# A Hymba-style block on one core: the filters' second stage a step later, the gates' scaling on VectorE, and a reordered pass change and filters' start

## The chip, the cores and the metric

The kernel runs on one core of a Trainium2 chip. The core has TensorE (PE, matrix products), VectorE (DVE), ScalarE (ACT), GpSimd (POOL) and SyncE (SP, which here only issues transfers), each with an instruction stream of its own that is worked through in order. The metric is the time of one execution in microseconds on the device; lower is better. The median of several runs is taken.

## The reference, cut to what matters

One encoder block, with 2048 positions, 1024 channels, float32. Half of the projected channels go through a Fourier mix, the other half through a Hyena operator of order 2, whose long filters are generated by a small network and normalised.

```
def implicit_filters(l, w0, b0, w_inner, b_inner, freq, w_out):
    z, t = positional_features(l)
    h = jnp.sin(fr * (z @ w0 + b0))
    for j in range(FILTER_INNER_LAYERS):
        h = jnp.sin(fr * (h @ w_inner[j] + b_inner[j]))
    h = (h @ w_out).reshape(l, HYENA_ORDER, N_DIRECTIONS, HYENA_WIDTH)
    h = h * decay[:, None, None, :]
    k = jnp.concatenate([h_fwd[:1] + h_bwd[:1], h_fwd[1:], jnp.zeros_like(h_fwd[:1]),
                         h_bwd[1:][::-1]], axis=0)
    return k * lax.rsqrt(jnp.sum(k * k, axis=0, keepdims=True) + EPS)

def hyena_mix(u, ...):
    u = short_conv(u, conv_w, conv_b)
    x1, x2, v = jnp.split(u, HYENA_ORDER + 1, axis=-1)
    k_freq = jnp.fft.rfft(implicit_filters(...), axis=0)
    z = v
    for n, gate in enumerate((x1, x2)):
        z = gate * fft_long_conv(z, k_freq[:, n], long_d[n])
    return z

def reference(x, ...):
    p = rmsnorm(x, g_mix) @ w_in
    u_f, u_h = p[..., :512], p[..., 512:]
    y_f = rmsnorm(fourier_mix(u_f), g_fourier)
    y_h = rmsnorm(hyena_mix(u_h, ...), g_hyena)
    x = x + jnp.concatenate([y_f, y_h], -1) @ w_out
    x = x + jnp.square(jax.nn.relu(rmsnorm(x, g_mlp) @ w_fc1)) @ w_fc2
    return rmsnorm(x, g_final)
```

## The kernel before, in words

**Stages.** In order of time: pass 1 of the input projection (x1 and x2, with the filter network between its groups), pass 2 (the Fourier part and v, with loads of tables and sums of weights between its groups), the filters with the Fourier mix in their first steps, Hyena, the output projection and the two layers of the MLP. The 2048 positions are 16 tiles of 128. The scheduler of the program fixes the order of each engine's instructions when the kernel is built, by the order of the code, by priorities and by what depends on what; `behind` adds a fixed "this after that".

**The projection (`project`, L337 to L458).** Each float32 operand is split into a high and a low half (`xh`, `xl`; `wh`, `wl`), and `mm3` (L208 to L212) makes three products of them. A group is one position tile times one half of the columns: 8 x 3 = 24 products into `pu`. `parts` gives the order of the groups, `front` loads and splits a tile's activations (L197 makes `xl`), and `weights_in` splits the weights. Where the weights carry a gain (`gmix`), the low half is made on VectorE by L200, else by L197. `convolve` runs the short convolution: `term` (L378) on VectorE, additions on GpSimd (L401, L405, L414) and, in `finish` (L397), on VectorE; the results go to the tensor `gates` in DRAM (0 is v, 1 and 2 are x1 and x2). In pass 2 the groups of the Fourier part are copied into `uf`.

**The filters (`filters`, L526 to L689).** There are eight units: four tiles of 128 channels times two orders n. A unit has four steps of each kind. `generate` (L566) multiplies the network's last layer into `pk`, VectorE multiplies by the decay (L568), ScalarE squares (L580), and GpSimd sums the squares into `acc` (L582 to L585). `stage1` (L625) is the first stage of the filter's Fourier transform, and VectorE transposes its result into `Gk` (L629). `stage2` (L634) multiplies `Gk` by the table `f2`; ScalarE copies the result to `ks` (L637, three buffers), and SyncE writes 1 MB of it to `spec` in DRAM (L641). `generate` and `stage1` take turns with two PSUM buffers each (`pair`). `normalise` (L590 to L600) sums `acc` over the partitions with a product, and works out the scale factors `sc`, `dk` and `both` on VectorE; `skip` (L607 to L613) puts the skip weight in and broadcasts the norms of a channel tile into `norms`.

**The order in the filters.** A loop of 43 steps runs all of it: step s has generate s of the 32, stage 1 of seven steps before, and stage 2 of eleven steps before, so a unit's first stage 2 stands in the step behind its last stage 1. `ordered` ties every product to the one before, so TensorE follows the code. In steps 0 to 10, `FOURIER` says how many steps of the Fourier mix come first: L482 multiplies `uf` into `pf`, and L464 transposes that into `Gf`. In steps 24 to 27 (`LOAD`) the four column tiles of v are fetched from `gates` into `zz`, 1 MB each, on SyncE's queue, and in `SCALE`'s steps GpSimd multiplies a tile by `norms` in four pieces (L688). The decay tiles of unit 0 are loaded over ScalarE's queue, at a raised priority.

**Hyena (`hyena`).** It reads `zz`, `gates` and, over SyncE's queue, the spectra (`ks<-spec`, L719); L733 is its first product, L748 and L756 follow.

## Time and profile before

| what | value |
|---|---|
| runs | 2293.11, 2289.97, 2285.28 us; median 2289.97 us |
| the profiled execution | 2289.12 us, span 2287.3 us |
| mean granted clock of TensorE | 0.989 |
| pass change | about 226 to 250 us into the span |
| filters, with the Fourier mix | about 406 to 612 us |
| DMA | 477.00 MB, mean 209 GB/s |

The time of an execution is a little more than its span, because the span begins with the first and ends with the last recorded instruction. In a timeline row the columns are start, duration, engine, line, operation, result and operands, tile shape and count; in brackets stands how long the engine was idle before and what ended that. In a row of windows come the stretch, busy time and instructions of each engine, the granted clock, the busy share of the DMA engines and GB/s. In a row of groups, the columns are busy time in all and mean ns of one, then the idle time ahead of them with what ended it.

### The profile page before, as it was taken

The numbers are of one execution on the slowest core, as the hardware profiler recorded it, in microseconds if no ns is written. First come the engines' busy times: TensorE is split into PE (matmuls) and PEld (weight loads), VectorE is DVE, ScalarE is ACT, GpSimd is POOL, SyncE is SP. The second block draws the span as 40 slices with busy tenths as digits, with TensorE's granted clock in tenths as the row PEclk, the third lists the DMA queues.
The fourth block names the chain that finished last, engine by engine and source line by source line (L and its number), as shares of the span: only waits on it lengthen the run. The fifth ranks groups of instructions, "written<-read, shape, count | busy, mean of one in ns | idle before, by whom it ended". The sixth has DMA issues, their size and how long they took to land.

```text
span 2287.3 us, 34559 instructions
## 1 busy us (share of the span) xinstructions
PE 2203.4 (96%) x12881; PEld 1801.2 (79%) x12881; DVE 1458.6 (64%) x2172; ACT 1076.4 (47%) x1788; POOL 788.1 (34%) x607
## 2 busy tenths in 40 slices
PE   8999999987899989998999999999999999999998
PEld 6888788665688858887888878888888888888886
DVE  6999767654478774457444465444476666866667
ACT  6545111453366564456555565555533333533334
POOL 3434333456276611136655556555300000000000
PEclk9999999998999999999999999999999999999999
DMA  8535986568886766567444475444499766866631
GB/s 271 179 130 182 355 284 238 178 245 269 333 257 206 218 190 180 177 210 238 158 152 152 152 242 173 152 152 152 143 335 339 237 195 192 304 193 195 192 119 74
DMA packets 296505, 477.00 MB, mean 209 GB/s; under 512 B 17349, under 2 KB 141455, under 8 KB 292113
## 3 DMA queue, kind: packets, MB, share of 16 engines
q1 hardware_dynamic: 290097, 458.29, 60.4%
q10 hardware_dynamic: 6240, 16.51, 2.1%
q8 instruction: 101, 1.65, 0.3%
q14 instruction: 67, 0.55, 0.1%
HBM read 305.17 MB, written 168.00 MB: 207 GB/s over the span
## 4 chain that ended last, share of the span: by engine, by line
PE 70%; POOL 2%; DVE 2%; DMA 2%; ACT 2%; issue 2%; SPq 0%; POOLq 0%; ACTq 0%; DVEq 0%
PE p2u L210 5%; PE p2u L212 5%; PE p2u L211 5%; PE p1u L210 5%; PE p1u L212 5%; PE p1u L211 5%; PE p2v L210 3%; PE p2v L212 3%; PE p2v L211 3%; PE pz L733 2%; PE p1v L211 2%; PE p1v L210 2%; PE p1v L212 2%; PE po L210 2%; PE po L212 2%; PE po L211 2%
## 5 line engine op out<-in xcount | busy, mean ns | idle before, releaser
L196 ACT CAST qahm<-ra 128x1024 fp32r<-128x1024 f32 x110 | 115.9, 1053 | 344.0 <-PE p2u L211 172.0
L197 DVE TENSOR_TENSOR qalm<-ra,qahm 128x1024 fp32r<-128x1024 f32 x110 | 134.7, 1224 | 154.0 <-ACT qahm L196 152.4
L1297 POOL TENSOR_TENSOR acc<-acc,gfin 128x512 f32<-128x512 f32 x4 | 5.1, 1277 | 631.6 <-DMA out<-acc 624.4
L211 PE MATMUL pu<-wl,xh 128*128 128x512 f32 x512 | 201.6, 394 | 4.2 <-DVE wl L200 4.0
L210 PE MATMUL pu<-wh,xh 128*128 128x512 f32 x512 | 204.1, 399 | 0.7 <-ACT wh L199 0.7
L212 PE MATMUL pu<-wh,xl 128*128 128x512 f32 x512 | 201.6, 394 | 1.9 <-DVE xl L197 1.9
L211 PE MATMUL p2u<-qblm,qahm 128*128 128x512 f32 x504 | 196.1, 389 | 0.0
L210 PE MATMUL p2u<-qbhm,qahm 128*128 128x512 f32 x504 | 195.8, 389 | 0.0
L212 PE MATMUL p2u<-qbhm,qalm 128*128 128x512 f32 x504 | 195.7, 389 | 0.0
L197 DVE TENSOR_TENSOR qblm<-rb,qbhm 128x1024 fp32r<-128x1024 f32 x110 | 134.0, 1218 | 3.8 <-ACT qbhm L196 3.5
L401 POOL TENSOR_TENSOR acc<-acc,cw 128x512 f32<-128x512 f32 x45 | 59.5, 1321 | 200.7 <-DVE acc L378 197.4
L196 ACT CAST ahm<-s 128x512 fp32r<-128x512 f32 x124 | 76.7, 621 | 98.5 <-PE p1v L211 54.0
L197 POOL TENSOR_TENSOR alm<-W,ahm 128x512 fp32r<-128x512 f32 x63 | 87.7, 1393 | 94.1 <-ACT ahm L196 94.1
L196 ACT CAST qbhm<-rb 128x1024 fp32r<-128x1024 f32 x110 | 115.3, 1048 | 5.9 <-DMA rb<-in_w_fc 3.1
L211 PEld LDWEIGHTS pu<-wl,xh 128*128 128x128 f32 x512 | 97.2, 190 | 26.1 <-DVE wl L200 5.5
L212 PEld LDWEIGHTS pu<-wh,xl 128*128 128x128 f32 x512 | 97.1, 190 | 23.3 <-DVE xl L197 3.4
L210 PEld LDWEIGHTS pu<-wh,xh 128*128 128x128 f32 x512 | 97.3, 190 | 21.5 <-ACT wh L199 1.1
L210 PEld LDWEIGHTS p2u<-qbhm,qahm 128*128 128x128 f32 x504 | 94.6, 188 | 20.0 <-issue 0.3
L212 PEld LDWEIGHTS p2u<-qbhm,qalm 128*128 128x128 f32 x504 | 94.6, 188 | 19.7
L211 PEld LDWEIGHTS p2u<-qblm,qahm 128*128 128x128 f32 x504 | 94.6, 188 | 19.6
L210 PE MATMUL p1u<-bm,ahm 128*128 128x512 f32 x252 | 99.8, 396 | 7.6 <-ACT ku L1159 7.6
L196 ACT CAST ahm<-W 128x512 fp32r<-128x512 f32 x94 | 57.8, 617 | 97.9 <-PE p1u L211 95.4
(375 smaller groups left out, 6159.8 us busy)
## 6 DMA issues: line engine op xcount, KB each, us to landing
W<-in_w_fc SPq DMA_DIRECT2D x66, 512.0 KB, 4.7
spec<-ks SPq DMA_DIRECT2D x32, 1024.0 KB, 5.4
ks<-spec SPq DMA_DIRECT2D x64, 512.0 KB, 4.6
rb<-td SPq DMA_DIRECT2D x64, 512.0 KB, 10.1
ra<-a1m SPq DMA_DIRECT2D x56, 512.0 KB, 3.7
ra<-a0m SPq DMA_DIRECT2D x54, 512.0 KB, 3.8
rb<-in_w_fc SPq DMA_DIRECT2D x46, 512.0 KB, 10.7
f<-in_w_fc SPq DMA_DIRECT2D x16, 1024.0 KB, 6.0
```

Of the source, the lines that this page charges most:

```text
L196: nc.scalar.copy(hi, src)
L197: (eng or nc.vector).tensor_sub(lo, src, hi)
L210: nc.tensor.matmul(o, lhsT=lh, rhs=rh, start=start, stop=False, skip_group_check=more)
L211: nc.tensor.matmul(o, lhsT=lh, rhs=rl, start=False, stop=False, skip_group_check=more)
L212: nc.tensor.matmul(o, lhsT=ll, rhs=rh, start=False, stop=stop, skip_group_check=more)
L401: nc.gpsimd.tensor_add(m1, m1, cw[:, 3, :])
L733: nc.tensor.matmul(p[:, 256 * sp : 256 * sp + 256], lhsT=e1[:, sp, :], rhs=zz[:, :, lo : lo + 16], start=True, stop=True)
L1297: nc.gpsimd.tensor_mul(acc[i][:, c], acc[i][:, c], gfin[:, c])
```

## The change

In the filters, stage 2 comes twelve steps behind generate instead of eleven, and the loop has 44 steps. The scaling of `zz` by `norms` goes from GpSimd to VectorE, one piece of a tile in each step from 28 on. The reciprocal and the factors `dk` and `both` move from `normalise` into a new `scales`, which stands behind the products of its step; the square root stays in `normalise`. A small fill of one row goes from GpSimd to VectorE.

At the filters' start, unit 0's first generate is split into `raw` (products) and `multiply`: its products come before the first four Fourier products, and its multiplication behind the fourth transposition. The last two groups of pass 2 are exchanged, so that the Fourier part's group is last, and unit 0's decay loads stand behind that group's copy into `uf`. At the pass change, the first four groups of pass 2 are tied to run one after the other, and the second tile's `front` has a raised priority.

```
@@ project
         else:
             parts[:4] = (0, 0), (1, 0), (0, 1), (1, 1)
+            parts[-2:] = (15, 1), (15, 0)
...
-            for k in range(8):
-                mm3(p, xh[:, k, :], xl[:, k, :], *w[h, k], k == 0, k == 7)
+            group = [mm3(p, xh[:, k, :], xl[:, k, :], *w[h, k], k == 0, k == 7) for k in range(8)]
+            if uf is not None and 0 < at < 4:
+                behind([group[0][0]], end)
+            end = group[-1][1]
             for j in after[at]:
-                fronts[j] = front(order[j])
+                with ExitStack() if uf is None or at else tc.high_priority(offset=200):
+                    fronts[j] = front(order[j])
...
-                nc.scalar.mul(uf[:, t, :], p, r)
+                filled = nc.scalar.mul(uf[:, t, :], p, r)
...
+        if uf is not None:
+            line.append(filled)
@@ ordered
-        if line:
-            behind([x], line[-1])
-        line[:] = [x]
+        if len(line) > 1:
+            behind([x], line.pop())
+        line.append(x)
@@ Unit.decay
-                (nc.scalar if self.i == 0 else nc.sync).dma_start(decs[k], A["decay"][self.ct][:, 8 * k : 8 * k + 8, :])
+                d = (nc.scalar if self.i == 0 else nc.sync).dma_start(decs[k], A["decay"][self.ct][:, 8 * k : 8 * k + 8, :])
+                if self.i == 0:
+                    behind([d], line[0])
             def generate(self, k):
+                self.multiply(k, self.raw(k))
@@ Unit.multiply
-                nc.vector.tensor_mul(new, p.rearrange(...), decs[k].rearrange(...))
+                made = nc.vector.tensor_mul(new, p.rearrange(...), decs[k].rearrange(...))
+                if first is not None:
+                    behind([made], first)
...
-                    nc.gpsimd.memset(end, 0.0)
+                    nc.vector.memset(end, 0.0)
@@ Unit.normalise
-                self.sc = rsqrt(v, fp, "k", 8)
+                self.root = fp.tile([P, 1], F32, tag="sq_k", name="sq_k", bufs=2)
+                nc.scalar.sqrt(self.root, self.v)
+
+            def scales(self):
+                v = self.v
+                self.sc = rsqrt(v, fp, "k", 8, self.root)
@@ the steps
-        SCALE = {28: 0, 30: 1, 32: 2, 38: 3}
-        for step in range(43):
+        for step in range(44):
...
+            if step == 0:
+                begun = units[0].raw(0)
             if step < SOLO:
                 for _ in range(FOURIER[step]):
-                    next(fourier_steps)
-            u, q = divmod(step - 11, 4)
+                    out = next(fourier_steps)
+            if step == 0:
+                units[0].multiply(0, begun, out)
+            u, q = divmod(step - 12, 4)
...
-            if u < 8:
+            if 0 < step < 32:
                 units[u].generate(k)
...
+            u, q = divmod(step - 5, 4)
+            if 0 <= u < 8 and q == 0:
+                units[u].scales()
...
-            if step in SCALE:
-                j = SCALE[step]
-                for q in range(4):
-                    z = zzs[0][:, 4 * q : 4 * q + 4, 128 * j : 128 * j + 128]
-                    nc.gpsimd.tensor_mul(z, z, norms[:, j : j + 1, :].broadcast_to([P, 4, 128]))
+            j, q = divmod(step - 28, 4)
+            if j >= 0:
+                z = zzs[0][:, 4 * q : 4 * q + 4, 128 * j : 128 * j + 128]
+                nc.vector.tensor_mul(z, z, norms[:, j : j + 1, :].broadcast_to([P, 4, 128]))
```

Where the instructions come to stand is decided when the program is built. First VectorE at the pass change, in the order of before: the numbers tell buffers apart, `wl_2313` and `wl_2319` are low halves of the last two Fourier weights, `wl_2323` that of the first v weight.

```order
L397 TENSOR_TENSOR acc<-acc,m_2215 128x512
L197 TENSOR_TENSOR wl_2313<-st_2314,wh_2312 128x512
L197 TENSOR_TENSOR wl_2319<-st_2314,wh_2318 128x512
L378 SCALAR_TENSOR_TENSOR acc<-pu_2219,nw_s,cw_270 128x512
L378 SCALAR_TENSOR_TENSOR m_2248<-pu_2219,nw_s,cw_270 128x512
L378 SCALAR_TENSOR_TENSOR m_2250<-pu_2219,nw_s,cw_270 128x512
L397 TENSOR_TENSOR acc<-acc,early 128x512
L397 TENSOR_TENSOR acc<-acc,m_2250 128x512
L397 TENSOR_TENSOR last<-last,nb 128x512
L200 SCALAR_TENSOR_TENSOR wl_2323<-st,gmix,wh_2322 128x512
```

The same stretch of VectorE in the changed kernel (its lines L382 and L401 are L378 and L397 of before):

```order
L401 TENSOR_TENSOR acc<-acc,m_2215 128x512
L197 TENSOR_TENSOR wl_2303<-st_2304,wh_2302 128x512
L197 TENSOR_TENSOR wl_2309<-st_2304,wh_2308 128x512
L197 TENSOR_TENSOR wl_2313<-st_2314,wh_2312 128x512
L382 SCALAR_TENSOR_TENSOR acc<-pu_2219,nw_s,cw_270 128x512
L197 TENSOR_TENSOR xl<-xc,xh 128x1024
L382 SCALAR_TENSOR_TENSOR m_2248<-pu_2219,nw_s,cw_270 128x512
L382 SCALAR_TENSOR_TENSOR m_2250<-pu_2219,nw_s,cw_270 128x512
L401 TENSOR_TENSOR acc<-acc,early 128x512
L401 TENSOR_TENSOR acc<-acc,m_2250 128x512
L401 TENSOR_TENSOR last<-last,nb 128x512
L197 TENSOR_TENSOR wl_2319<-st_2314,wh_2318 128x512
```

The split of an activation tile (`xl`) has moved ahead, and the last Fourier weight's low half (`wl_2319`) stands behind the three additions of `finish`.

Second, TensorE around the first stage 2 of unit 0, before (L566 generate, L625 stage 1, L634 stage 2):

```order
L612 MATMUL pdiag<-diag,ones 128x128
L566 MATMUL pk<-wo,emb 32x128 x32
L625 MATMUL pk_4386<-k,e1k 32x512 x8
L634 MATMUL pk_4401<-Gk,f_2585 128x128 x4
L634 MATMUL pk_4408<-Gk,f_2585 128x128 x4
```

And in the changed kernel (there L578, L648 and L657):

```order
L635 MATMUL pdiag<-diag,ones 128x128
L578 MATMUL pk<-wo,emb 32x128 x32
L648 MATMUL pk_4386<-k,e1k 32x512 x8
L578 MATMUL pk<-wo,emb 32x128 x32
L648 MATMUL pk_4444<-k,e1k 32x512 x8
L657 MATMUL pk_4455<-Gk,f_2585 128x128 x4
L657 MATMUL pk_4462<-Gk,f_2585 128x128 x4
```

One generate and one stage 1 now stand between a unit's last stage 1 and its first stage 2.

Third, VectorE in steps 22 to 24 before, the products with the decay and the transpositions:

```order
L629 STREAM_TRANSPOSE Gk<-pk_5262 128x8x2x32 x2
L568 TENSOR_TENSOR k<-pk,dec_4737 128x8x8x16
L629 STREAM_TRANSPOSE Gk<-pk_5333 128x8x2x32 x2
L568 TENSOR_TENSOR k<-pk,dec 128x8x8x16
L576 TENSOR_TENSOR k<-k,lag_5394 1x8x16
L629 STREAM_TRANSPOSE Gk<-pk_5402 128x8x2x32 x2
```

And in the changed kernel, where L715 is the scaling (`dec_4723`, `pk_5319` and so on are the same buffers under new numbers):

```order
L652 STREAM_TRANSPOSE Gk<-pk_5248 128x8x2x32 x2
L583 TENSOR_TENSOR k<-pk,dec_4723 128x8x8x16
L715 TENSOR_TENSOR zz<-zz,norms 128x4x128 x2
L652 STREAM_TRANSPOSE Gk<-pk_5319 128x8x2x32 x2
L715 TENSOR_TENSOR zz<-zz,norms 128x4x128 x2
L583 TENSOR_TENSOR k<-pk,dec 128x8x8x16
L593 TENSOR_TENSOR k<-k,lag_5380 1x8x16
L594 MEMSET k 1x8x16
L652 STREAM_TRANSPOSE Gk<-pk_5388 128x8x2x32 x2
```

The first tile's four scalings, which on GpSimd stood behind sums of squares, stand two and two around the transpositions of step 23; the second and third tiles' eight follow in the same way over steps 25 and 26, and the fourth tile's four stand near the end of the filters.

More of the change, by code (lines that the diff above doesn't have):

```diff
@@ L208, in mm3, with rsqrt @@
     def mm3(o, lh, ll, rh, rl, start, stop, more=False):
-        nc.tensor.matmul(o, lhsT=lh, rhs=rh, start=start, stop=False, skip_group_check=more)
+        a = nc.tensor.matmul(o, lhsT=lh, rhs=rh, start=start, stop=False, skip_group_check=more)
         nc.tensor.matmul(o, lhsT=lh, rhs=rl, start=False, stop=False, skip_group_check=more)
-        nc.tensor.matmul(o, lhsT=ll, rhs=rh, start=False, stop=stop, skip_group_check=more)
-    def rsqrt(v, pl, nm, keep=None):
-        s, r = (pl.tile(list(v.shape), F32, tag=f"{a}_{nm}", name=f"{a}_{nm}") for a in ("sq", "rc"))
+        return a, nc.tensor.matmul(o, lhsT=ll, rhs=rh, start=False, stop=stop, skip_group_check=more)
+    def rsqrt(v, pl, nm, keep=None, s=None):
+        r = pl.tile(list(v.shape), F32, tag=f"rc_{nm}", name=f"rc_{nm}")
         q = pl.tile(list(v.shape), F32, tag=f"nw_{nm}{keep or ''}", name=f"nw_{nm}", bufs=keep)
-        nc.scalar.sqrt(s, v)
+        if s is None:
+            s = pl.tile(list(v.shape), F32, tag=f"sq_{nm}", name=f"sq_{nm}")
+            nc.scalar.sqrt(s, v)
         nc.vector.reciprocal(r, s)
@@ L335, in weights_in @@
         return w
+    line = []
     def project(ip, fx, cps, sets, uf):
@@ L482, in fourier @@
             ordered(nc.tensor.matmul(p, lhsT=e1f, rhs=ufv[:, :, :, 16 * c : 16 * c + 16], start=True, stop=True))
-            turned(G, c, p.rearrange("p (x c e) -> p c e x", c=8, e=2))
-            yield
+            yield turned(G, c, p.rearrange("p (x c e) -> p c e x", c=8, e=2))
         def rows(i):
@@ L566, in generate, with multiply @@
                                 ordered(nc.tensor.matmul(o, lhsT=w, rhs=wo[rows[h], self.n, cols], start=True, stop=True))
+                return p
+            def multiply(self, k, p, first=None):
                 new = self.k.rearrange("p c l j -> p l c j")[:, 8 * k : 8 * k + 8]
-                nc.vector.tensor_mul(new, p.rearrange("p q (l c j) -> p (q l) c j", l=4, c=8), decs[k].rearrange("p l (c j) -> p l c j", c=8))
+                made = nc.vector.tensor_mul(new, p.rearrange("p q (l c j) -> p (q l) c j", l=4, c=8), decs[k].rearrange("p l (c j) -> p l c j", c=8))
+                if first is not None:
+                    behind([made], first)
                 if self.n == 1 and self.i < 7:
```

6 lines of the change are left out of this document (3 added, 3 removed).

## The prediction

> **What bounds the kernel now.** I read the page's first part first: which engine has no time to spare.
>
> ```profile
> PE 2203.4 (96%) x12881; PEld 1801.2 (79%) x12881; DVE 1458.6 (64%) x2172; ACT 1076.4 (47%) x1788; POOL 788.1 (34%) x607
> ```
>
> TensorE is busy for 2203.4 of 2287.3 us. The change takes no matrix product away, so it can only win from the 84 us in which TensorE idles, and from stretches in which it works at a reduced clock. Next I read the waits of TensorE over the whole run (columns: engine, tile and line that waits, engine, tile and line it waits for, us in total, how often, longest).
>
> ```profile
> PE psum_k L590 <- POOL acc L585: 14.1, 4, 10.1
> PE pk L634 <- ACT sqr L580: 8.9, 5, 1.8
> PE pk L634 <- DVE Gk L629: 4.9, 3, 1.8
> PE pu L211 <- DVE wl L200: 4.0, 1, 4.0
> PE pv L756 <- POOL y L748: 3.6, 1, 3.6
> PE pf L482 <- DVE Gf L464: 3.5, 1, 3.5
> ```
>
> These six rows, 39.0 us, are what the edits address: the norm product behind GpSimd's sum of squares, the filters' second stage (L634, eight waits), the pass change, Hyena's start and the filters' start. Third, the windows behind the long waits, because a wait may cost more than its own length (columns: us, busy us and instructions by engine, granted clock, DMA share, GB/s).
>
> ```profile
> 236.00:241.00 5.00, 5.00 (x12) 3.93 (x13) 5.00 (x8) 2.10 (x4) 0.00 (x0) 0.50 0.98 366
> 415.00:420.00 5.00, 5.00 (x8) 1.97 (x8) 3.70 (x7) 1.04 (x4) 0.00 (x0) 0.66 0.38 141
> 542.00:547.00 5.00, 5.00 (x96) 3.65 (x96) 2.44 (x9) 2.10 (x5) 2.02 (x3) 0.72 0.35 120
> ```
>
> Behind the waits of 3.95, 3.50 and 10.12 us the granted clock is 0.50, 0.66 and 0.72, with TensorE busy all 5 us. The third stretch alone loses 5.00 x (1 - 0.72) = 1.4 us.
>
> The Trainium skill, page "TensorE: Matmul & The Clock Gate", section "What's actually happening", says that TensorE falls to half its clock after at least one idle window of about 3.4 us. The three rows agree; by that rule each new wait of that length costs such a stretch again, which the sum below charges from the 1.4 us in any case.
>
> A time of mine is compared with 0.3% of this kernel, 6.9 us, about what a measurement can tell from no change.
>
> **A, the pass change (about 226 to 250 us).**
>
> ```profile
> 227.64 1.28 DVE L197 TENSOR_TENSOR wl<-st,wh 128x512 fp32r<-128x512 f32 x2
> 231.66 0.39 PE L210 MATMUL pu<-wh,xh 128*128 128x512 f32 x1
> 232.35 1.73 DVE L397 TENSOR_TENSOR acc<-acc,early 128x512 f32<-128x512 f32 x1 [1.46 <-POOL acc L405]
> 235.21 5.37 DVE L200 SCALAR_TENSOR_TENSOR wl<-st,gmix,wh 128x512 fp32r<-128x512 f32 x8
> 236.00 0.79 PE L211 MATMUL pu<-wl,xh 128*128 128x512 f32 x1 [3.95 <-DVE wl L200]
> ```
>
> The timeline shows before: TensorE stops at 232.05 until VectorE, which had waited for GpSimd's sum and then done three additions, makes the first low half of the v weights at 235.21. Now the groups run whole, so the first asks for no v weight. But in VectorE's new order the last Fourier weight's low half stands behind those same three additions; before, it was made with its neighbour at 227.64, 0.64 us each. It would now be made from 235.21 to 235.85, and the 23rd of the first group's 24 products wants it at about 231.4. That is a stall of 4.4 us in place of 3.95, with the slow clock behind it as before. The v weights have the whole second Fourier group to be made in. I take **-0.5 us** (minus is a loss). Bounds: -3, should the v weights be late as well; +6.5 if VectorE were early and the stall and its slow clock (3.95 + 5.00 x 0.50) vanished.
>
> **B, the filters' start.**
>
> ```profile
> 406.41 0.82 ACTq L545 DMA_DIRECT2D dec<-in_decay  x2
> 406.69 3.70 PE L482 MATMUL pf<-uf,e1f 128*128 128x512 f32 x8
> 413.00 1.21 DVE L568 TENSOR_TENSOR k<-pk,dec 128x1024 f32<-128x1024 f32 x1
> 414.98 5.37 PE L482 MATMUL pf<-uf,e1f 128*128 128x512 f32 x8 [3.50 <-DVE Gf L464]
> 420.27 1.16 PE L566 MATMUL pk<-wo,emb 64*32 64x128 f32 x64
> ```
>
> Before, the first filter products stand behind the first Fourier ones and TensorE waits 3.50 us for a transposition; the next eight Fourier products take 5.37 us where eight took 3.70. Putting the 1.16 us of filter products first, and the last projection group on the Fourier part, gives VectorE those 3.5 us. Removed: 3.50 + (5.37 - 3.70) = 5.2 us. What can be late next is the decay: its load, now behind the last projection result, follows by about 1 us, and from load issue (406.41) to the product that uses it (413.00) lie at most 6.6 us, against some 4 us now; that bounds the loss at 2.6. I take **+5 us**, range 2.5 to 5.5.
>
> **C, the second stage a step later.**
>
> ```profile
> 465.65 1.16 PE L566 MATMUL pk<-wo,emb 64*32 64x128 f32 x64
> 469.58 1.16 PE L566 MATMUL pk<-wo,emb 64*32 64x128 f32 x64
> 519.36 1.31 DVE L629 STREAM_TRANSPOSE Gk<-pk 128x512 f32<-128x512 f32 x2
> 520.81 2.02 PE L634 MATMUL pk<-Gk,f 128*128 128x128 f32 x16 [1.79 <-ACT sqr L580]
> 605.17 7.39 PE L634 MATMUL pk<-Gk,f 128*128 128x128 f32 x64 [1.57 <-DVE Gk L629]
> 613.98 1.07 ACT L637 COPY ks<-pk 128x512 f32<-128x512 f32 x2 [2.58 <-DMA spec<-ks]
> 590.00:600.00 10.00, 8.45 (x93) 6.13 (x96) 3.94 (x6) 3.31 (x6) 4.32 (x4) 1.00 1.01 408
> ```
>
> A step takes 469.58 - 465.65 = 3.93 us. Before, each unit's first second-stage product stands directly behind the last first-stage product whose transposition it reads (520.81, 605.17); eight such waits, 8.9 + 4.9 = 13.8 us. With a whole step between, the two transpositions, 1.31 us, are long done, and the waits go. What is late next is the end: the last unit's second stage runs alone for five steps instead of four, 1.85 us each (7.39 / 4), and each writes 1 MB, which at 408 GB/s takes 2.6 us; the copy at 613.98 already waits 2.58 us for such a write. So the last two waits (2 x 1.57 = 3.1) may come back. I take **+12.3**, the middle of 10.7 and 13.8.
>
> **D, the scaling moved from GpSimd to VectorE.**
>
> ```profile
> 517.91 1.12 PE L625 MATMUL pk<-k,e1k 64*32 64x512 f32 x16
> 519.16 4.89 SPq L682 DMA_DIRECT2D zz<-gates  x2
> 529.14 5.00 POOL L688 TENSOR_TENSOR zz<-zz,norms 128x512 f32<-128x512 f32 x4 [6.21 <-DMA zz<-gates]
> 541.38 0.59 PE L590 MATMUL psum_k<-ones,acc 128*128 128x1 f32 x2 [10.12 <-POOL acc L585]
> 544.89 0.52 SPq L682 DMA_DIRECT2D zz<-gates  x1
> 553.37 5.00 POOL L688 TENSOR_TENSOR zz<-zz,norms 128x512 f32<-128x512 f32 x4 [2.81 <-DMA zz<-gates]
> 565.05 0.40 PE L590 MATMUL psum_k<-ones,acc 128*128 128x1 f32 x2 [3.00 <-POOL acc L585]
> 460.00:520.00 60.00, 52.86 (x1252) 38.24 (x1251) 36.24 (x64) 30.63 (x67) 33.60 (x32) 1.00 0.70 257
> ```
>
> Before, GpSimd waits for the gates' transfer, scales for 5 us at a time, and the sums queued behind it keep TensorE waiting 10.12 and 3.00 us. All of L590's 14.1 us go with it, and the slow stretch of 1.4: removed 15.5.
>
> Added: the same wait on VectorE, which works in order. The first two scalings now stand between the product of step 23 and that step's transpositions. The transfer is issued at 519.16, right behind the first stage of step 22, and its data are there at 529.14, 9.98 us on. On TensorE that first stage ends at 517.91 + 1.12 = 519.03; then come 2.02 + 1.16 + 1.12 for step 23 (second stage, filter products, first stage) and 2.02 + 1.16 for step 24, so the first stage of step 24 is due at 526.5. It needs the buffer that step 23's two transpositions empty: 529.14 + 2 x 0.7 + 1.3 = 531.9. Stall: 5.4, and behind it a slow stretch, 1.4.
>
> The price of a scaling on VectorE is not in the trace; the nearest rows of its size, 128x512, are these.
>
> ```profile
> L770 DVE TENSOR_TENSOR zz<-pb,xg 128x512 f32<-128x512 f32 x32 | 21.3, 685 | 7.5 <-PE pb L769 6.9
> L397 DVE TENSOR_TENSOR acc<-acc,m 128x512 f32<-128x512 f32 x42 | 53.3, 1270 | 0.5
> ```
>
> 0.69 us with one operand from PSUM; 1.27 with both from SBUF, which this has. GpSimd is busy for 33.60 of 60 us around here, so I take 1.0. Twelve of the sixteen fall into steps 23 to 27: 12 us, while VectorE has (60 - 36.24) / 60 = 40% of 5 x 3.93 us free, 7.8. The rest, about 4, lands on TensorE (0.5 at 0.69; 7.4 at 1.27). The third tile's transfer, issued some two steps (7.9 us) ahead of its scaling, took 553.37 - 544.89 = 8.5 before; with queues as they are I charge 2 (0 to 4). Net: 15.5 - 5.4 - 1.4 - 4 - 2 = **+2.7 us**, range -4 to +8.
>
> The Trainium skill, page "SBUF — State Buffer", section "Who interferes with whom", speaks against this edit: VectorE's second port is GpSimd's own, and the loser of the lock waits for it entirely. L397's 1.27 against 0.69 agrees, and its first rival below is what that rule would do in full.
>
> **E and F.** Hyena's first spectrum load waits, before, for the last spectrum write on its queue; in the new order it needs only the writes of its own tile.
>
> ```profile
> 621.94 2.79 SPq L719 DMA_DIRECT2D ks<-spec  x4
> 631.20 1.01 PE L756 MATMUL pv<-y,f 128*128 128x128 f32 x3 [3.62 <-POOL y L748]
> ```
>
> The wait of 3.62 us at Hyena's start hangs on those loads; with the clock behind it, up to 5 us; but the writes themselves end no sooner. I take **+2**, range 0 to 5. The scale factors "behind the products" cost nothing either way: VectorE's order has them where they stood, ahead of the product. The small fill moved from GpSimd is eight instructions of one row, hidden in VectorE's 40% of free time; without that cover, at most the 0.69 us of a far larger tile in L770's row, 5.5 in all.
>
> **Sum.** -0.5 + 5 + 12.3 + 2.7 + 2 = 21.5. The profiled execution took 2289.12 (span 2287.3), so 2267.6; the median of before, 2289.97, lies 0.85 above that execution: **2268.5 us**.
>
> **Rivals.**
> 1. *VectorE becomes the bound of steps 23 to 28.* Should a scaling cost what the addition at 232.35 cost, 1.73, the twelve take 8.8 us more: 2277. For: both operands in SBUF, GpSimd at work. Against: 42 of L397's kind average 1.27. 0.15.
> 2. *No new stall.* The gates' transfer comes in time, because GpSimd's own delay no longer holds the queues, and the pass change is free: 5.4 + 1.4 + 2 from D, 7.0 from A: 2253. For: the two transfers were issued together with 4.89 us of issue time. Against: VectorE's order at both places. 0.10.
> 3. *The writes bound the filters.* Each step writes 1 MB, and 590 to 600 shows the DMA engines at 1.01 of their time; then what TensorE gains in C to E waits for transfers, and A and B alone remain: 2285.5, no difference that shows. Against: 460 to 520 moves 257 GB/s only. 0.07.
> 4. *Slower.* VectorE in order makes the filters wait for the gates: every us that the transfer lands later than 9.98 costs one at the first tile and one at the third, two in all. The 21.5 us are used up at 9.98 + 10.7 = 20.7 us, and beyond 24 us the kernel is slower by over 0.3%; at 26 it would take 2300. For: the spectrum writes share the queue. Against: 9.98 and 8.5 were the landings here. 0.04.
>
> **How the numbers follow.** The forecast has 0.64, its own range 2258 to 2278 by the terms' bounds. The range of 8 in 10 takes in the first rival and half of the way to the second: 2255 to 2281. Faster by over 0.3% (below 2283.1): forecast, rivals 1 and 2, less a little of their tails, 0.87; within 0.3%: the third and those tails, 0.09; slower 0.04.
>
> **What would show it.** Right: no wait of the second stage for Gk or squares; none of the norm product; one wait of TensorE of about 5 us in step 24 ending on VectorE's transpositions behind zz; a wait of about 4.4 us in the first projection group of pass 2 for a low half of a weight; no 3.5 us wait at the filters' start. Wrong: scalings at 0.7 or 1.7 us, a gates transfer far from 10 us, or TensorE waiting for copies that wait for spectrum writes before the last five steps.

## The result and the profile after

The changed kernel takes 2276.32 us in the median (2271.93 to 2279.59), the kernel before 2290.81 in the same comparison; the ratio is 0.994, with a 95% interval from 0.9921 to 0.9958. So it is faster, by 14.5 us, 0.6%. The time lies in the forecast range (2255 to 2281); the gain is a third smaller than the 21.5 us that were forecast, and the parts were further off than their sum. Two executions in the table below, 2786.02 us of e3 and 4484.02 us of e12, took far longer than the others of their kernel and are left out of medians and ratios.

The profiled execution of the changed kernel took 2276.27 us, with a span of 2274.5. First its engines, then the waits of TensorE over the whole run (engine, tile and line that waits, what it waits for, us in total, times, longest). Line numbers have moved: L648 is stage 1, L652 its transposition, L657 stage 2, L607 the norm product, L490 the first Fourier product, L474 its transposition.

```profile
PE 2204.1 (97%) x12881; PEld 1800.7 (79%) x12881; DVE 1470.5 (65%) x2196; ACT 1074.3 (47%) x1788; POOL 768.9 (34%) x583
```

```profile
PE pk L648 <- DVE Gk L652: 7.5, 2, 4.6
PE pu L211 <- DVE wl L197: 6.5, 1, 6.5
PE pv L783 <- POOL y L775: 3.5, 1, 3.5
PE pf L490 <- ACT longd L539: 3.5, 1, 3.5
PE pf L490 <- DVE Gf L474: 2.0, 1, 2.0
PE psum_k L607 <- POOL acc L602: 1.0, 2, 0.7
```

Stage 2 (L657) waits for Gk or squares no longer, 13.8 us before. The norm product waits 1.0 us in place of 14.1. In their place stand waits of 7.5 us in stage 1, 6.5 at the pass change and 5.5 at the filters' start. To see what each stretch gave, I compare when the same product starts in the two traces (minus is earlier):

| product | before | changed | difference | since the row above |
|---|---|---|---|---|
| transposition of `dk8`, just behind pass 2 | 406.54 | 408.49 | +1.95 | +1.95 |
| filter products of step 10 | 459.90 | 464.95 | +5.05 | +3.10 |
| Hyena's first product | 612.40 | 598.28 | -14.12 | -19.17 |
| first product of L756 (now L783) | 631.20 | 616.91 | -14.29 | -0.17 |
| end of the span | 2287.3 | 2274.5 | -12.8 | +1.5 |

In these two traces the pass change lost 1.95 us, the start 3.1, the rest of the filters won 19.17, and Hyena's start won nothing.

**The pass change.** The timeline of the changed kernel (start, duration, engine, line, operation, result and operands, count, and in brackets the idle time before and what ended it), its GpSimd, VectorE and TensorE rows:

```profile
229.59 1.21 DVE L197 TENSOR_TENSOR xl<-xc,xh 128x1024 fp32r<-128x1024 f32 x1
229.75 2.18 POOL L405 TENSOR_TENSOR acc<-acc,cw 128x512 f32<-128x512 f32 x1 [3.10 <-DVE acc L382]
233.31 1.73 DVE L401 TENSOR_TENSOR acc<-acc,early 128x512 f32<-128x512 f32 x1 [1.18 <-POOL acc L409]
236.17 0.68 DVE L197 TENSOR_TENSOR wl<-st,wh 128x512 fp32r<-128x512 f32 x1
236.90 0.79 PE L211 MATMUL pu<-wl,xh 128*128 128x512 f32 x1 [6.51 <-DVE wl L197]
```

TensorE waits 6.51 us for the last Fourier weight's low half, which stands behind the three additions as the order said. It is made at 236.17, later than the 235.21 that the prediction took from before. The split that moved ahead (229.59) runs beside GpSimd's addition, which takes 2.18 us; in the trace of before the same addition took 1.30 (229.66), and the group of that line has a mean of 1.33. So GpSimd's sums, and VectorE behind them, are 0.96 us later (233.31 against 232.35).

**The start of the filters.** ScalarE's instructions and its queue, and the rows of VectorE and TensorE that wait:

```profile
408.65 10.38 ACTq L552 DMA_DIRECT2D dec<-in_decay  x4
416.65 0.71 DVE L474 STREAM_TRANSPOSE Gf<-pf 128x512 f32<-128x512 f32 x1
419.07 0.17 ACT L539 COPY longd<-plongd 128x8 f32<-128x8 f32 x1 [9.79 <-DMA gates<-last]
419.29 3.63 PE L490 MATMUL pf<-uf,e1f 128*128 128x512 f32 x4 [3.45 <-ACT longd L539]
424.81 0.61 ACT L497 ACTIVATE neg<-ff 128x128 f32<-128x128 f32 x2 [5.57 <-DMA ff<-in_ff]
425.45 0.30 ACT L592 COPY lag<-k 1x128 f32<-1x128 f32 x1
425.78 0.28 DVE L593 TENSOR_TENSOR k<-k,lag 1x128 f32<-1x128 f32 x1 [8.42 <-ACT lag L592]
427.08 2.84 PE L490 MATMUL pf<-uf,e1f 128*128 128x512 f32 x6 [2.02 <-DVE Gf L474]
```

All four decay loads now issue from ScalarE's queue at 408.65, and it takes 10.38 us until the last is issued; the copy `longd` behind them ends its wait with the write of the last tile of v. Then `neg`, the sign copy of the first Fourier table, waits for that table until 424.81. The table is also fetched later: its load (`ff<-in_ff`) is issued at 418.09 on SyncE's queue, and at 413.61 before. Before, `lag` stood ahead of `neg`:

```profile
414.24 0.30 ACT L575 COPY lag<-k 1x128 f32<-1x128 f32 x1 [6.79 <-DVE k L568]
419.15 0.62 ACT L490 ACTIVATE neg<-ff 128x128 f32<-128x128 f32 x2 [3.96 <-issue]
```

Here it stands behind, and VectorE waits 8.42 us for `lag` in front of three transpositions that TensorE needs.

**The scaling.** Timeline of steps 23 to 28 in the changed kernel, and the group of all scalings (busy us in all, mean ns of one):

```profile
525.11 1.55 DVE L715 TENSOR_TENSOR zz<-zz,norms 128x512 f32<-128x512 f32 x2 [4.37 <-DMA zz<-gates]
526.58 1.30 DVE L652 STREAM_TRANSPOSE Gk<-pk 128x512 f32<-128x512 f32 x2
528.03 1.63 PE L648 MATMUL pk<-k,e1k 64*32 64x512 f32 x16 [4.64 <-DVE Gk L652]
537.79 3.14 DVE L715 TENSOR_TENSOR zz<-zz,norms 128x512 f32<-128x512 f32 x3
543.03 1.72 DVE L715 TENSOR_TENSOR zz<-zz,norms 128x512 f32<-128x512 f32 x1 [0.96 <-DMA zz<-gates]
545.90 1.85 DVE L715 TENSOR_TENSOR zz<-zz,norms 128x512 f32<-128x512 f32 x3
546.12 1.96 PE L648 MATMUL pk<-k,e1k 64*32 64x512 f32 x16 [2.84 <-DVE Gk L652]
...
L715 DVE TENSOR_TENSOR zz<-zz,norms 128x512 f32<-128x512 f32 x16 | 12.7, 834 | 6.7 <-DMA zz<-gates 5.3 <-ACT norms L636 1.3
```

VectorE stops for the transfer, then scales, then transposes, and the first stage of step 24 waits 4.64 us (5.4 were forecast), a later one 2.84. Behind both waits TensorE runs at a reduced clock: 0.66 over 528 to 533 us, and 0.50 over 546 to 551. A scaling takes about 0.65 us where GpSimd is idle (545.90 has three in 1.85); three that meet GpSimd's additions take 0.94 (the second of 525.11), 1.77 (the second of 537.79) and 1.72 (543.03). The mean is 0.83, the median 0.68.

### The profile page after: what moved, and what is told of

Read it like the earlier page. It is cut to its first block, busy times and chain, and to the rows that moved or that the text cites. A ratio compares the mean times of both kernels' runs of the same rounds, so it can differ in the third digit from the quotient of the medians.

```text
span 2274.5 us, 34533 instructions
## 1 busy us (share of the span) xinstructions
PE 2204.1 (97%) x12881; PEld 1800.7 (79%) x12881; DVE 1470.5 (65%) x2196; ACT 1074.3 (47%) x1788; POOL 768.9 (34%) x583
## 4 chain that ended last, share of the span: by engine, by line
PE 85%; DVE 4%; DMA 4%; ACT 3%; POOL 2%; issue 2%; ACTq 0%; SPq 0%; DVEq 0%; POOLq 0%
PE p2u L210 5%; PE p2u L212 5%; PE p2u L211 5%; PE p1u L212 5%; PE p1u L210 5%; PE p1u L211 5%; PE pu L212 4%; PE pu L211 4%; PE pu L210 4%; PE p2v L210 3%; PE p2v L212 3%; PE p2v L211 3%; PE pk L657 2%; PE p1v L210 2%; PE pz L760 2%; PE p1v L212 2%
```

## The experiments

Each is the changed kernel with one edit, unless it says otherwise. The ratio is to the kernel of before in the same comparison; on that scale the changed kernel stands at 0.994 (0.9921 to 0.9958). The last column is the start of Hyena's first product in the profiled execution. The kernel of before took 2290.13 to 2292.41 us in these comparisons, so a difference between two medians of the table is good to a us or two only. The start of the filters shifts too: seven kernels with the products of the changed one up to there begin the product behind pass 2 between 407.31 (e5) and 409.06 us (e6). Where it matters I count from that product.

| run | median us | ratio (95%) | Hyena's first product |
|---|---|---|---|
| before | 2290.81 | 1 | 612.40 |
| changed | 2276.32 | 0.9940 (0.9921 to 0.9958) | 598.28 |
| e1 start as before | 2270.56 | 0.9909 (0.9886 to 0.9932) | 594.06 |
| e2 two decay loads early | 2275.77 | 0.9931 (0.9916 to 0.9947) | 598.00 |
| e3 scalings tied late | 2273.53 | 0.9916 (0.9897 to 0.9936) | 592.86 |
| e4 weights' splits first | 2268.64 | 0.9902 (0.9885 to 0.9920) | 591.09 |
| e5 lag ahead of neg | 2266.60 | 0.9891 (0.9869 to 0.9913) | 591.78 |
| e6 scale factors behind | 2282.03 | 0.9961 (0.9948 to 0.9975) | 602.95 |
| e7 stage 2 as before | 2296.89 | 1.0025 (1.0015 to 1.0036) | 617.18 |
| e8 scaling on GpSimd | 2278.39 | 0.9942 (0.9925 to 0.9960) | 601.88 |
| e9 before, stage 2 later alone | 2275.19 | 0.9936 (0.9919 to 0.9953) | 596.99 |
| e10 three repairs | 2258.70 | 0.9860 (0.9843 to 0.9877) | 581.72 |
| e11 two repairs | 2264.07 | 0.9883 (0.9864 to 0.9902) | 588.60 |
| e12 pass change as before | 2276.66 | 0.9935 (0.9918 to 0.9951) | not shown |

### e1: the filters' start put back

```
-            parts[-2:] = (15, 1), (15, 0)
-                if self.i == 0:
-                    behind([d], line[0])
-            if step == 0:
-                begun = units[0].raw(0)
-            if step == 0:
-                units[0].multiply(0, begun, out)
-            if 0 < step < 32:
+            if step < 32:
```

> The changed kernel with the filters' start put back as it was: last two groups of pass 2 in their old order, the filter products of step 0 behind the first four Fourier products, unit 0's decay loads tied to nothing. Theory (the new start costs time: between the end of pass 2 and the second generate the changed kernel takes 2.9 us more than before, because ScalarE's queue holds longd, neg and lag behind the four decay loads): about 3 us faster than the changed kernel, some 2273 us, no wait of a Fourier product for longd, and the wait of 3.5 us for Gf back. Rival (the new start gains the 5 us of the prediction and the loss seen in the trace came from the pass change shifting the loads): about 5 us slower, some 2281 us.

The wait for `longd` is gone and the old one is back. The row is a wait of TensorE in this kernel (L489 is the first Fourier product):

```profile
PE pf L489 <- DVE Gf L473: 3.5, 1, 3.5
```

The filter products of step 3 start at 431.26 in place of 434.57, Hyena's first product 4.2 us earlier, and the median lies 5.8 us under that of the changed kernel; the intervals of the ratios still touch. The theory holds in the trace: this part of the change, as built, costs time.

### e2: two decay loads free to be early

```
-                if self.i == 0:
+                if self.i == 0 and k < 2:
                     behind([d], line[0])
```

> The changed kernel with only the first two of unit 0's four decay loads tied behind the last projection result; the other two are free to be issued early, as before the change. Theory (the fourth decay load waits on ScalarE's queue for the write of the last tile of v, and longd, neg and lag stand behind it): longd is copied within 1 us of its product, the 3.45 us wait for it and the slow stretch behind it go, and the second generate starts 4 to 7 us earlier: about 2271 us. Rival (ScalarE is held by the load of the first Fourier table, which is late on SyncE's queue in any case): the wait moves to neg and lag, and less than 2 us is won.

The second generate starts at 417.40, 5.45 us earlier, and no product waits for `longd`. But the third starts at 429.81 against 429.86. First the row of ScalarE's timeline in this kernel, then that of TensorE's waits:

```profile
422.67 0.61 ACT L497 ACTIVATE neg<-ff 128x128 f32<-128x128 f32 x2 [12.62 <-DMA ff<-in_ff]
```

```profile
PE pf L490 <- DVE Gf L474: 5.3, 1, 5.3
```

ScalarE now waits 12.62 us for the table in one piece, and what was won turns into a wait of 5.3 us for Gf. The median is 0.6 us lower, no difference. The rival holds. The decay loads were a wait in front of another one.

### e3: each scaling behind its own step's transposition

```
-                    nc.vector.transpose(dst, src)
+                    latest[:] = [nc.vector.transpose(dst, src)]
...
-                nc.vector.tensor_mul(z, z, norms[:, j : j + 1, :].broadcast_to([P, 4, 128]))
+                scaled = nc.vector.tensor_mul(z, z, norms[:, j : j + 1, :].broadcast_to([P, 4, 128]))
+                behind([scaled], latest[0])
```

> The changed kernel with each scaling on VectorE tied behind the last transposition of its own step, so that none is pulled ahead to steps 23 to 26. Theory (the stalls of 4.64 and 2.84 us in steps 24 and 28 come from scalings that wait in order for their transfer): both stalls go and with them the slow stretches behind, some 4 us more; 9 to 12 us faster than the changed kernel, about 2265 us; a scaling takes 0.7 to 1.3 us. Rival (VectorE is the bound there by its load): the waits for Gk come back later, spread over steps 28 to 38, and less than 3 us is won.

Neither wait for Gk is left, and Hyena starts 5.4 us earlier; the median falls by 2.8 only, and the intervals overlap (the profiled execution, 2269.43 us, is the fastest of the three). Theory and rival each have a part: the 7.5 us of stalls are gone, and 3.3 us (0.6 in the changed kernel) come back as waits of the filter products to which the trace gives no releaser. From the product behind pass 2 to Hyena's first, TensorE idles 14.6 us in place of 17.2, and the same products take 169.7 us in place of 172.6: about half of what is won is clock (0.99 in the mean in place of 0.96). The first row is a wait of TensorE in this kernel, the second the scalings by shape, ns min/median/max.

```profile
PE pk L578 <- issue: 3.3, 3, 1.9
...
L715 DVE TENSOR_TENSOR zz<-zz,norms x16: 647/666/1554, 547.6 to 588.2; 128x512 f32<-128x512 f32 x16
```

### e4: the Fourier weights' splits first

```
                 if s < 0:
-                    split(hi, lo, t)
+                    with tc.high_priority(offset=60):
+                        split(hi, lo, t)
```

> The changed kernel with a raised priority for the splits of the Fourier weights, so that the last low half stands ahead of the last additions of pass 1 on VectorE. Theory (the 6.51 us wait in the first group of pass 2 is for this low half alone): it goes, with the slow stretch behind it, and pass 2 starts its second group 6 us earlier: 6 to 9 us faster than the changed kernel, about 2268 us. Rival (the next low halves, those of the v weights, or the second tile's low half are as late): a wait of 3 to 6 us stands in the second or third group instead, and 0 to 3 us is won.

The 6.51 us wait is gone; the row is the wait of TensorE at the pass change that is left.

```profile
PE pu L212 <- DVE xl L197: 2.4, 1, 2.4
```

The first filter products start at 403.66 in place of 409.33, Hyena 7.2 us earlier, and the median falls by 7.7. The theory holds; of the rival, the second tile's low half is late by 2.4 us.

### e5: lag ahead of neg

The edit of e2, and besides:

```
-            nc.scalar.mul(neg, ffs[i][:, :, 1], -1.0)
+            turned_sign = nc.scalar.mul(neg, ffs[i][:, :, 1], -1.0)
+            behind([turned_sign], squared[1])
...
-                    nc.scalar.square(sq..., new[:, 4 * q : 4 * q + 4])
+                    squared.append(nc.scalar.square(sq..., new[:, 4 * q : 4 * q + 4]))
```

> The changed kernel with two of unit 0's decay loads free to be early (as in the run before) and, besides, the sign copy of the first Fourier table (neg) tied behind unit 0's first squares on ScalarE. Theory (the start loses its gain because neg, which waits for a table that lands at 422 to 425, stands ahead of lag on ScalarE, VectorE's addition of lag waits for that, and the transpositions of Gf queue behind it): the waits for longd and Gf both go, the second generate starts near 417.4 and the third near 422 instead of 429.9: 6 to 8 us faster than the changed kernel, about 2269 us. Rival (the Fourier part needs the table at that time anyway): the wait moves to the first products that use neg, and less than 3 us is won.

The theory holds. ScalarE's rows of this kernel and the third generate on TensorE:

```profile
408.84 0.17 ACT L540 COPY longd<-plongd 128x8 f32<-128x8 f32 x1 [0.73 <-DVE acc L401]
415.98 0.30 ACT L593 COPY lag<-k 1x128 f32<-1x128 f32 x1 [6.98 <-DVE k L584]
422.56 0.62 ACT L497 ACTIVATE neg<-ff 128x128 f32<-128x128 f32 x2 [5.63 <-issue]
```

```profile
421.02 1.16 PE L579 MATMUL pk<-wo,emb 64*32 64x128 f32 x64
```

No Fourier product waits now, neither for `longd` nor for Gf. From the product behind pass 2 to step 3 this kernel takes 425.74 - 407.31 = 18.4 us; before took 429.71 - 406.54 = 23.2, the changed kernel 434.57 - 408.49 = 26.1. So by step 3 the gain of some 5 us that the prediction saw in this part is there, once `lag` is not behind `neg`. Most of it does not last. The norm product of the first unit now waits for GpSimd's sum in step 5 (0.7 us at most for one such wait in the changed kernel):

```profile
434.63 0.38 PE L608 MATMUL psum_k<-ones,acc 128*128 128x1 f32 x2 [2.21 <-POOL acc L603]
```

By step 10 this kernel has taken 459.00 - 407.31 = 51.7 us, before 53.4. And e1, which is the same kernel with the old start, takes 53.5 to step 10 and 185.7 to Hyena's first product, where e5 takes 184.5: the new start, once repaired, is worth 1 to 2 us. The median of e5 is 9.7 us under that of the changed kernel, Hyena's start 6.5 earlier, of which 1.2 lie ahead of the filters.

### e6: the scale factors really behind the products

```
-                self.sc = rsqrt(v, fp, "k", 8, self.root)
+                self.sc = rsqrt(v, fp, "k", 8, self.root, products[-1])
...
-        nc.vector.reciprocal(r, s)
+        x = nc.vector.reciprocal(r, s)
+        if first is not None:
+            behind([x], first)
```

> The changed kernel with the scale factors tied behind the product with the decay on VectorE, which the change's code says and its built order does not do. Theory (VectorE's seven small operations, 1.6 us, ahead of the product make TensorE wait where the next products need the buffer): 0.3 to 0.7 us for each of eight units, 2 to 5 us faster, about 2273 us. Rival (the chain is covered by VectorE's free time): within 1 us of the changed kernel in the trace, no difference that shows.

Neither came. The median is 5.7 us higher than that of the changed kernel, with intervals that just overlap, and Hyena starts 4.7 us later, because the factor `dk` is late for the product that uses it in the next step (TensorE's waits of this kernel, L633 is that product):

```profile
PE pdk L633 <- DVE dk L622: 6.5, 5, 3.9
```

That the built order of the change left the factors ahead of the products was the better place.

### e7: stage 2 as before

```
-            u, q = divmod(step - 12, 4)
+            u, q = divmod(step - 11, 4)
```

> The changed kernel with stage 2 again eleven steps behind generate; all else as changed. Theory (the eight waits of 13.8 us come back; one or two of them are covered by the writes at the end): Hyena's first product starts 11 to 14 us later than in the changed kernel, about 2289 us. Rival (the stalls in steps 24 to 28 overlap with two of the eight waits, or the spectrum writes set the end): 5 to 9 us, about 2283 us.

It costs more than either said: Hyena starts 18.9 us later, and the median is 20.6 us higher, slower than before the change.

```profile
PE pk L657 <- DVE Gk L652: 11.0, 4, 5.2
PE pk L657 <- ACT sqr L597: 7.2, 4, 1.8
```

Eight waits again, but 18.2 us long in place of 13.8: with the scalings on VectorE a transposition can be up to 5.2 us late, and stage 2 directly behind it waits for that too, in place of stage 1, whose 7.5 us are gone. In all, from the product behind pass 2 to Hyena, TensorE idles 33.1 us against 17.2 in the changed kernel, and its products take 3.4 us longer. The two edits lean on each other.

### e8: the scaling on GpSimd

```
-            j, q = divmod(step - 28, 4)
-            if j >= 0:
+        SCALE = {28: 0, 30: 1, 32: 2, 38: 3}
...
-                nc.vector.tensor_mul(z, z, norms[:, j : j + 1, :].broadcast_to([P, 4, 128]))
+            if step in SCALE:
+                j = SCALE[step]
+                for q in range(4):
...
+                    nc.gpsimd.tensor_mul(z, z, norms[:, j : j + 1, :].broadcast_to([P, 4, 128]))
```

> The changed kernel with the scaling back on GpSimd in the steps of before. Theory (moving it is worth what GpSimd's delay cost, 14.1 us of waits and some slow clock, less the stalls of 4.64 and 2.84 us on VectorE and the slow clock behind those): 4 to 6 us slower than the changed kernel, about 2281 us, with a wait of the norm product of some 10 us. Rival (with stage 2 later TensorE has other work behind GpSimd's sum): as fast as the changed kernel within 2 us.

```profile
PE psum_k L607 <- POOL acc L602: 12.4, 4, 7.8
```

The waits of the norm product are back, 12.4 us, and those for Gk are not there. Hyena starts 3.6 us later, 4.2 when counted from the product behind pass 2 (407.89 here); the median is 2.1 higher, which the intervals don't part from the changed kernel. The trace takes the theory's side, at the low end of its 4 to 6; the times don't decide.

### e9: before, with stage 2 later and nothing else

```
-            u, q = divmod(step - 11, 4)
+            u, q = divmod(step - 12, 4)
-        for step in range(43):
+        for step in range(44):
```

> The kernel of before with the filters' second stage a step later and nothing else of the change. Theory (stage 2 a step later is the one part that carries the gain, since the pass change and the start together lost about 5 us and the scaling's move gave 2 to 4): Hyena's first product starts 13 to 16 us earlier than before, about 2276 us, as fast as the whole change. Rival (the step later needs the scaling on VectorE, because GpSimd's delay else takes its place): 7 to 10 us faster than before, about 2282 us.

The theory holds: 2275.19 us, as fast as the whole change. Hyena starts 15.4 us earlier than before. From the product behind pass 2 to there this kernel takes 189.57 us, the changed kernel 189.79: taken together, the other edits in the filters win nothing as built. No wait of stage 2 for Gk or squares is left, and the norm product's waits, though GpSimd still scales, are somewhat shorter than the 14.1 us of before:

```profile
PE psum_k L590 <- POOL acc L585: 12.5, 4, 8.4
```

### e10 and e11: the repairs together

e10 has the edits of e3, e4 and e5; e11 those of e4 and e5.

> The changed kernel with three repairs together: the Fourier weights' splits at a raised priority, the sign copy behind unit 0's first squares with two decay loads free, and each scaling tied behind the transposition of its own step. Theory (the three losses lie in different stretches and add up: 6 to 8, 8 to 10 and 3 to 6 us): 15 to 20 us faster than the changed kernel, about 2259 us. Rival (what is won before the filters' end is given back there, to the spectrum writes or the transfers of v): 9 to 12 us, about 2266 us, no faster than the best of the repairs alone.

> The same without the third repair, the scalings where the change has them. Theory: the stalls of some 4.7 and 2.8 us in steps 24 to 28 stay, so 4 to 6 us slower than the kernel with all three, about 2264 us. Rival (tying the scalings only moves the waits): within 2 us of the kernel with all three.

Both theories hold. e10 takes 2258.70 us, 1.4% under the kernel of before and faster than the changed kernel with intervals well apart; e11 takes 2264.07. The third repair is worth 5.4 us, more than alone; between the product behind pass 2 and Hyena it takes 3.9 us from TensorE's idle time and 2.9 from its products, whose mean clock there is 1.00 in e10 and 0.96 in e11. What TensorE still waits for in e10 between 200 and 650 us, the longest rows:

```profile
PE pk L580 <- issue: 4.1, 3, 1.7
PE pv L786 <- POOL y L778: 3.0, 1, 3.0
PE pu L212 <- DVE xl L197: 2.6, 2, 2.4
PE psum_k L609 <- POOL acc L604: 2.0, 2, 1.2
```

### e12: the pass change put back

```
-            if uf is not None and 0 < at < 4:
-                behind([group[0][0]], end)
...
-                with ExitStack() if uf is None or at else tc.high_priority(offset=200):
-                    fronts[j] = front(order[j])
+                fronts[j] = front(order[j])
```

> The changed kernel with the pass change as it was: no fixed order of the first four groups of pass 2 and no raised priority for the second tile's loads and split. Theory (the reordered pass change costs 2 us: a wait of 6.5 us for the last Fourier weight's low half in place of one of 4.0 us for the first v weight's): the wait of 4.0 us is back, the filters' first product starts about 2 us earlier in the trace, and the time is 2 us below the changed kernel, some 2274 us, which five rounds may not tell from none. Rival (the new order is worth the slow clock behind the wait, so that undoing it loses as much as it wins): the filters start within 0.5 us of the changed kernel, or later.

Inconclusive. Its profiled execution is the one of 4484.02 us, with TensorE busy for 4465.0 of them, so that its trace shows no wait that could be compared, and the other times, 2270.26 to 2280.76, surround those of the changed kernel. Neither theory nor rival is shown.

## Why the prediction was right in direction and range, and too high in size

That the time fell into the range is in part luck: the start of the filters came out 8.1 us worse than forecast (-3.1 against +5), and the second stage 4 us better (16.3 against 12.3). The prediction's own range, 2258 to 2278, is also narrower than the sums of its terms' bounds, 2251.2 to 2283.8.

**A, the pass change** (forecast -0.5). The mechanism was right: the wait for the last Fourier weight's low half. It was undersized: 6.5 us against 4.4. The low half is there about 1 us later than reckoned, because GpSimd's addition took 2.18 us beside the split that had moved ahead, and the prediction took GpSimd's sums at their old time; and the product asks for it at 236.90 - 6.51 = 230.39, about 1 us before the 231.4 of the prediction. Of the 1.95 us lost at the end of pass 2 less is certain: before and e9, which share their code up to there, stand at 406.54 and 407.42, and the seven kernels with the products of the changed one at 407.31 to 409.06, 408.25 in the mean. So the loss is about 1 us, and the direct test of it, e12, settled nothing. e4 shows that the wait was that one low half.

**B, the filters' start** (forecast +5, range 2.5 to 5.5). This step failed; the trace has -3.1. The prediction looked at the queue of the decay loads alone and priced the loads' landing, not what stands behind them on ScalarE. The failed sentence is "What can be late next is the decay". What was late next was `longd` behind the loads, and behind that `lag`: multiplying behind the fourth transposition put `lag` behind `neg`, and `neg` waits for a table. e2 shows that the decay loads were not the last wait, e5 that the order of `lag` and `neg` was, e1 that undoing this part wins time; the order of `lag` and `neg` was not changed alone. The size was wrong as well. Of the 5.2 us that the prediction took for removed, e5 has 23.2 - 18.4 = 4.8 by step 3, but 1.7 by step 10, where part has come back as a wait for GpSimd's sum.

**C, the second stage a step later** (forecast +12.3). Right, and too small. e9, which has this part alone, starts Hyena 15.4 us earlier, and 16.3 from the product behind pass 2 on (it is 0.88 later there). All 13.8 us of waits went; the fear that the last two would come back as waits for the spectrum writes didn't come true, since the time from the last generate to Hyena's first product fell in the changed kernel, from 35.18 us (577.22 to 612.40) to 33.76 (564.52 to 598.28). The rest is accounted for in the two traces: between those two products TensorE idles 19.3 us in place of 33.5, which is 14.2, and the same products take 170.2 us in place of 172.4, which is 2.1. With the scaling on VectorE the part is worth more, 18.9 by e7.

**D, the scaling** (forecast +2.7). The net was about right, and that is in part luck, because the terms were not. By e8 the part is worth 3.6 to 4.2 us in the trace; by the difference to e9 from step 10 on, where e9 wins 152.5 - 135.5 = 17.0, it is 19.2 - 17.0 = 2.2. The two stalls were forecast at 5.4 and 2 and are 4.64 and 2.84. The 4 us charged for VectorE's load show as no wait of their own: beside the two stalls TensorE waits 0.9 us in all for VectorE's products with the decay. The median of a scaling, 0.68, is even one of the prediction's signs of being wrong (1.0 was taken). In return the slow clock behind the stalls was charged once, at 1.4 us, and came twice: 5 x 0.34 + 5 x 0.50 = 4.2 us by the windows above. The errors largely cancel.

**E and F** (forecast +2 and nothing). Hyena's start won 0.17: the wait there is 3.5 us as before. As the prediction says, it hangs on the spectrum loads: ScalarE's copy ahead of it waits for them in both traces, first before, then changed.

```profile
626.90 0.29 ACT L722 COPY ks<-ks 1x128 f32<-1x128 f32 x1 [11.85 <-DMA ks<-spec]
612.61 0.29 ACT L749 COPY ks<-ks 1x128 f32<-1x128 f32 x1 [11.23 <-DMA ks<-spec]
```

The first of these loads is now issued 604.38 - 598.28 = 6.1 us behind Hyena's first product, in place of 9.5 (621.94), but the copy starts 14.3 us behind it, in place of 14.5. So the earlier issue was there, and brought no earlier landing; why is not shown. The factors cost nothing because they had not moved; moved in earnest, in e6, they cost 5.7.

Behind L756's first product 1.5 us were lost again. That is no effect that can be told from none: from Hyena's first product to the end of the span, where the experiments edit nothing, their traces take 1673.5 (e1) to 1677.9 us (e7), before 1674.9, changed 1676.2.

Of the rivals, the first (a scaling at 1.73 us) was wrong on average, though single scalings took 1.72 and 1.77. Of the second (no new stall), the norm product's waits did shrink to 1.0 us, but both new stalls came. The writes, the third, did not bound the filters. The fourth needed a later landing, and the first tile was there 525.11 - 516.49 = 8.6 us after its load was issued (9.98 in the prediction).

## What to carry to other kernels

Where an edit reorders one engine, read what stands behind each moved instruction on every engine that it waits for or that waits for it: the start was lost on the decay loads and, behind them, on a small sign copy on ScalarE that the diff does not touch. A wait that is removed is worth its length only if the next one on that path is read too: e2 removed a wait of 3.45 us, and the next one grew from 2.0 to 5.3. Nor is a gain in one step a gain of the stage: of e5's 4.8 us by step 3, 1.7 were left by step 10. And where a scheduler sets the order, the built order has to be read, and an operation that waits for a transfer needs its place fixed: changing the order in three places took the time from 2276.32 to 2258.70 us, more than the whole change had won.

## What the runs showed of the hardware

A scaling of 128x512 on VectorE with both operands in SBUF took about 0.65 us with GpSimd idle, and 0.94 to 1.77 where it met GpSimd's additions; GpSimd's addition took 2.18 us beside VectorE's split against a mean of 1.33 on its line. The Trainium skill, page "SBUF — State Buffer", section "Who interferes with whom", describes an exclusive lock between the two on a shared pair of ports; these rows agree, and they show that either side can be the one that waits. In the changed kernel TensorE's granted clock was 0.52 over the 5 us behind the wait of 6.51 us, 0.67 behind 3.45, 0.66 behind 4.64 and 0.50 behind 2.84, a shorter wait than any of the three in the prediction; behind the wait of 2.02 us it was 1.00. The 16 products of stage 1 took 1.63 us behind the stall of 4.64 and 1.96 behind that of 2.84, in place of 1.12.
